# The last feed-forward by Strassen's 2x2 block product, with the closing norm on turned token tiles

## The chip, the cores and the metric

The kernel runs on one core of one Trainium2 chip. The metric is the device time of one execution in microseconds. Engines are TensorE (PE, with its weight loads as PEld), VectorE (DVE), ScalarE (ACT), GpSimd (POOL) and SyncE (SP), whose queue issues most DMAs.

## The reference, cut to what matters

Two layers, 1024 tokens of width 1024, all in float32. Layer 0 has a short gated convolution, layer 1 an attention with forget gates; each layer ends with a gated feed-forward of hidden width 2816, and each sub-layer with a norm.

```python
D_MODEL, SEQ, D_FF = 1024, 1024, 2816

def swiglu(h, w_gate, w_up, w_down):
    return (jax.nn.silu(h @ w_gate) * (h @ w_up)) @ w_down

for l in range(2):
    sh1, sc1, g1, sh2, sc2, g2 = jnp.split(c_act @ w_ada[l] + b_ada[l], 6, axis=-1)
    h = x * (1 + sc1) + sh1
    y = short_conv_mixer(h, ...) if l == 0 else forgetting_attention(h, ...)
    x = layer_norm(ALPHA * x + g1 * y, ln1_g[l], ln1_b[l])
    h = x * (1 + sc2) + sh2
    y = swiglu(h, ffn_w_gate[l], ffn_w_up[l], ffn_w_down[l])
    x = layer_norm(ALPHA * x + g2 * y, ln2_g[l], ln2_b[l])
```

## The kernel before, in words

Activations lie features on partitions: `x[k, half]` is 128 features by 512 tokens. Every large product splits both operands into a rounded part and the rest and adds three products (`mm3`, L166; its matmuls are L169 to L171), each 128x128 weights by 128x512. SBUF is cut into 47 pages of 512 KB, lent between classes ("h", "w", "hid", "att", and "f" for the Strassen stages); PSUM has six banks for products and two small ones. What stands where on each engine's queue is set by a recording layer that orders the program's steps by priority and data; `weave` mixes two lists of steps.

The first feed-forward (`first_ffn`, `hidden`, `down`) uses a Strassen form with seven products M1 to M7 for two by two blocks. The hidden width is taken in 11 pairs of 128-feature blocks. In `hidden`, a slot is one product of one pair for gate (m = 0) and up (m = 1), 12 matmuls each. For the first six pairs (`NEARLY`) M1 and M2 run ahead, in 12 slots that are woven with the norm's second half; the other slots follow. Blocks of weights come through a list of loads (`lq`), are added on GpSimd (L918 to L923), split by `split_f` (L659 on ScalarE, L660 on VectorE), and the activation sums T are made once by `sums_tail` (L681 to L745). `out` adds what is needed to a bank, applies SiLU to the gate and multiplies it with up:

```python
                nc.vector.tensor_tensor(y, bank, other, op=ALU.add)     # L999
                gp.tensor_tensor(y, y, a, op=ALU.mult)                  # L1000
```

`derive` makes the differences of hidden blocks that the down product needs (GpSimd, L1008), and `store` (L868) writes them to DRAM from SyncE's queue. From slot 28 on, each slot also loads a page of modulation weights and multiplies it in on VectorE (`ada_slot`, L260 and L262). `down` reloads the hidden blocks in three chunks and adds each of seven products times four row blocks to x (L1321).

The last feed-forward (`last_ffn`) has the plain form. Gate and up are taken block by block (`expand`), `ffn_evac` multiplies (L391 to L393). After the first chunk, x is turned to tokens on partitions (`to_token_major`, 64 transposes, L1375), so that the down product (`token_item`, L1400) and the closing norm (`token_norm`) work on 128 tokens by 512 features: per token tile two squares with their sums on ScalarE (L1423), the power on GpSimd (L1427, L1428), scale and shift on VectorE (L1417, L1434), or for one half ScalarE (L1437) and GpSimd. Its weights go through `Weights` (L147 and L153). Between attention and this stage, `self.rest` holds the last items of attention's output product (L423) and the first half's norm; the second half's norm (`ln_steps(1, ltail)`) is woven into the first products.

## Time and profile before

| | us |
|---|---|
| median of 3 runs | 2519.61 (2512.10 to 2519.83) |
| the profiled execution | 2518.77 |
| its span, first to last instruction | 2517.0 |
| TensorE busy | 2400.4 (95%) |
| VectorE busy | 1497.8 (60%) |
| ScalarE, GpSimd busy | 827.3 (33%), 860.0 (34%) |
| mean granted clock of TensorE | 0.981 of full speed |

Busy times are of one profiled execution; the program's own time is its span and a little around it. Matmuls overlap, so the busy time of a group of matmuls is more than the time that they hold the engine.

### The profile page before, as it was taken

What the parts mean: (1) busy time and instruction counts of PE and PEld (TensorE: products, weight loads), DVE (VectorE), ACT (ScalarE), POOL (GpSimd) and SP (SyncE); (2) the same over time, 40 slices, a digit from 0 to 9 for tenths busy, and PEclk for the clock granted to TensorE, in tenths of its full rate; (3) what the DMA queues carried; (4) which work ended last, traced back from release to release, by engine and by line L of the source; (5) the groups of instructions that cost most, each with busy time, mean ns of one, the idle gap of its engine ahead of it and who ended that gap; (6) DMA issues with size and microseconds to landing.
All of it is one profiled execution on the core that took longest, in us unless ns stands there. A gap on an engine that the chain in (4) does not pass through costs nothing. (4 is left out here: it accounts for less than half of the span.)

```text
span 2517.0 us, 29595 instructions
## 1 busy us (share of the span) xinstructions
PE 2400.4 (95%) x10905; PEld 1948.8 (77%) x10905; DVE 1497.8 (60%) x2129; ACT 827.3 (33%) x1321; POOL 860.0 (34%) x686
## 2 busy tenths in 40 slices
PE   7899999898899999999999999999999999999997
PEld 5688887687778878777777777777788888888886
DVE  5654548856788878986464667897632223232326
ACT  3311105421232333434223666665521111212113
POOL 6300002675556452343000556557330202030304
PEclk9999999999999999999999999999999999999999
DMA  8333303655575774215557555652211111111101
GB/s 269 118 101 117 92 17 97 202 163 173 174 225 173 272 249 147 83 51 194 192 179 226 174 176 145 153 133 72 67 34 51 51 51 51 51 43 50 44 32 67
DMA packets 286645, 311.95 MB, mean 124 GB/s; under 512 B 16068, under 2 KB 198548, under 8 KB 286500
## 3 DMA queue, kind: packets, MB, share of 16 engines
q1 hardware_dynamic: 274884, 284.69, 37.1%
q10 hardware_dynamic: 11616, 25.37, 2.7%
q8 instruction: 86, 1.41, 0.2%
q14 instruction: 59, 0.48, 0.1%
HBM read 252.91 MB, written 57.08 MB: 123 GB/s over the span
## 5 line engine op out<-in xcount | busy, mean ns | idle before, releaser
L169 PE MATMUL mm<-pg,pg 128*128 128x512 f32 x3004 | 1188.8, 397 | 35.8 <-DVE tA L979 11.4
L170 PE MATMUL mm<-pg,pg 128*128 128x512 f32 x3004 | 1186.1, 395 | 14.5 <-DVE pg L370 7.2
L171 PE MATMUL mm<-pg,pg 128*128 128x512 f32 x3004 | 1183.8, 394 | 3.6 <-POOL pg L368 2.6
L169 PEld LDWEIGHTS mm<-pg,pg 128*128 128x128 f32 x3004 | 571.7, 190 | 161.7 <-issue 18.2
L170 PEld LDWEIGHTS mm<-pg,pg 128*128 128x128 f32 x3004 | 571.8, 190 | 136.2 <-DVE pg L370 10.0
L171 PEld LDWEIGHTS mm<-pg,pg 128*128 128x128 f32 x3004 | 571.3, 190 | 125.2 <-POOL pg L368 4.1
L159 ACT CAST pg<-pg 128x1024 fp32r<-128x1024 f32 x144 | 150.5, 1052 | 586.2 <-PE mm L170 301.1
L660 DVE TENSOR_TENSOR pg<-pg,pg 128x1024 fp32r<-128x1024 f32 (+1 forms) x161 | 245.5, 1535 | 59.0 <-ACT pg L659 34.3
L1402 POOL TENSOR_TENSOR pg<-pg,tB 128x512 f32<-128x512 f32 x80 | 107.6, 1346 | 463.0 <-DVE tB L1400 462.1
L659 ACT CAST pg<-pg 128x1024 fp32r<-128x1024 f32 (+1 forms) x161 | 159.7, 1013 | 285.6 <-DVE pg L660 81.6
L163 DVE TENSOR_TENSOR pg<-pg,pg 128x1024 fp32r<-128x1024 f32 x124 | 154.2, 1248 | 151.9 <-ACT pg L159 149.4
L393 DVE TENSOR_TENSOR tB<-mm,tA 128x512 f32<-128x512 f32 x44 | 30.4, 692 | 215.9 <-PE mm L171 215.7
L262 DVE SCALAR_TENSOR_TENSOR ga<-pg,cact,ga 128x512 f32<-128x512 f32 x119 | 115.0, 966 | 53.9 <-DMA pg<-in_w_ada_dram 40.3
L1400 DVE TENSOR_TENSOR tB<-mm,pg 128x512 f32<-128x512 f32 x96 | 66.2, 690 | 134.7 <-PE mm L171 134.6
L1788 POOL TENSOR_SCALAR pg<-pg,st 128x512 f32<-128x512 f32 (+7 forms) x128 | 97.9, 773 | 122.1 <-DVE st L1786 116.3
L1811 DVE TENSOR_TENSOR pg<-sm,pg 128x512 fp32r<-128x512 f32 x192 | 104.1, 551 | 26.6 <-ACT pg L1810 23.8
L1810 ACT CAST pg<-sm 128x512 fp32r<-128x512 f32 x192 | 89.0, 480 | 50.8 <-PE sm L1807 48.7
L1785 ACT ACTIVATE pg<-s,st 128x512 f32<-128x512 f32 (+7 forms) x128 | 94.5, 744 | 28.3 <-DVE st L1782 19.1
L1779 DVE TENSOR_REDUCE st<-s 128x1 f32<-128x1024 f32 (+3 forms) x96 | 91.2, 951 | 15.1 <-PE s L1773 14.5
L1807 PE MATMUL sm<-ident,pg 128*128 128x128 f32 x576 | 98.6, 276 | 1.6 <-POOL pg L1788 1.3
L1190 POOL TENSOR_TENSOR pg<-pg,pg 128x1024 f32<-128x1024 f32 (+1 forms) x24 | 61.6, 2574 | 100.5 <-DVE pg L660 38.9
L1819 PE MATMUL mm<-pg,pg 128*128 128x512 f32 x192 | 80.3, 418 | 5.9 <-ACT pg L1810 4.7
(217 smaller groups left out, 2376.5 us busy)
## 6 DMA issues: line engine op xcount, KB each, us to landing
pg<-in_w_ada_dram SPq DMA_DIRECT2D x68, 512.0 KB
scr_hid<-pg SPq DMA_DIRECT2D x77, 256.0 KB
pg<-scr_hid SPq DMA_DIRECT2D x35, 512.0 KB
g<-in_w_ada_dram SPq DMA_DIRECT2D x56, 256.0 KB
pg<-in_ffn_w_gate_dram SPq DMA_DIRECT2D x56, 256.0 KB
pg<-in_ffn_w_up_dram SPq DMA_DIRECT2D x56, 256.0 KB
pg<-in_conv_w_in_dram SPq DMA_DIRECT2D x24, 512.0 KB
pg<-in_ffn_w_down_dram SPq DMA_DIRECT2D x44, 256.0 KB
```

What stands on the lines that cost most here:

```text
L159: nc.scalar.copy(hi, raw)
L163: nc.vector.tensor_tensor(lo, raw, hi, op=ALU.subtract)
L169: mm(out, lhsT=whi, rhs=xhi, start=first, stop=False, skip_group_check=skip)
L170: mm(out, lhsT=whi, rhs=xlo, start=False, stop=False, skip_group_check=skip)
L171: mm(out, lhsT=wlo, rhs=xhi, start=False, stop=last, skip_group_check=skip)
L262: eng.scalar_tensor_tensor(acc, w, s, acc, op0=ALU.mult, op1=ALU.add)
L659: nc.scalar.copy(hi[:, 0:n], flat[:, 0:n])
L660: nc.vector.tensor_tensor(lo[:, 0:n], flat[:, 0:n], hi[:, 0:n], op=ALU.subtract)
L1402: nc.gpsimd.tensor_tensor(z, z, m, op=ALU.add)
L1788: nc.gpsimd.tensor_scalar(lg[:, i], lg[:, i], s[:, i:i + 1], 1.0, op0=ALU.mult, op1=ALU.mult)
L1807: nc.tensor.transpose(p[:, j * P:(j + 1) * P], lg[j][:, kt * P:(kt + 1) * P], self.c["ident"])
L1811: nc.vector.tensor_tensor(pt[:, 1, a:], p[:, a:], pt[:, 0, a:], op=ALU.subtract)
```

## The change

The last feed-forward uses the same Strassen code as the first: `ffn_ahead` and `ffn_run` are the former `first_ffn_ahead` and the first part of `first_ffn`, now for layer l. x stays features on partitions to the end; `token_steps` turns each token tile after its last update, gets the mean by a product with a column of 1/1024 and norms the tile out of PSUM. The first token half's norm is woven with the last eight products, the second half's follows the last product. In `out` and `derive`, which both feed-forwards use, GpSimd's multiplications and differences go to VectorE. Layer 1 has no modulation slots.

```diff
@@ out, derive (in hidden, both layers)
-                gp.tensor_tensor(y, y, a, op=ALU.mult)
+                nc.vector.tensor_tensor(y, y, a, op=ALU.mult)
...
             def tt(n, o, a, b, op=ALU.subtract):
-                gp.tensor_tensor(o, a, b, op=op)
-                if n:
-                    store(n, j, o)
+                nc.vector.tensor_tensor(o, a, b, op=op)
+                store(n, j, o)
@@ run (in hidden)
-            queue(2, len(slots), self.adaq_lq((len(slots) - nada) // 4))
+            queue(2, len(slots), self.adaq_lq((len(slots) - nada) // 4) if l == 0 else [])
...
-                if i >= nada:
+                if i >= nada and l == 0:
                     self.ada_slot()
@@
-    def first_ffn_ahead(self):
+    def ffn_ahead(self, l):
         for k in range(KD):
-            self.drop("h", self.h.pop((k, 1)))
-        self.gather("h", "w", "raw")
+            if (k, 1) in self.h:
+                self.drop("h", self.h.pop((k, 1)))
+        self.gather("h", "w", "raw") if l == 0 else self.gather("h")
...
-        self.hidden_begin, self.hidden_run = self.hidden(0, NEARLY, False)
+        self.hidden_begin, self.hidden_run = self.hidden(l, NEARLY, False)
         self.hidden_begin()
@@
-    def to_token_major(self, half):
...
-    def token_item(self, half, t, c, ck, fs, gate, last):
...
-    def token_norm(self, half, t, sums, G, B, end):
...
+    def token_steps(self, half, t, G, B, mean, bank, end):
...
+        def turn():
+            box["p"] = [bank(), bank()]
+            for k in range(KD):
+                x = self.x[k, half][:, tok]
+                nc.tensor.transpose(box["p"][k // 4][:, k % 4 * P:(k % 4 + 1) * P], x, self.c["ident"])
+            for k in range(KD):
+                nc.tensor.matmul(mean[:, t:t + 1], lhsT=self.x[k, half][:, tok], rhs=self.c["ones"][:, 0:1],
+                                 start=k == 0, stop=k == KD - 1)
         def stats():
...
+            nc.vector.tensor_scalar(nm, mean[:, t:t + 1], -1.0, None, op0=ALU.mult)
             for c in range(2):
                 m = self.t("tmp", [P, HALF], tag="tA", bufs=3)
-                nc.scalar.activation(m, zs[c], AF.Square, bias=nm, accum_out=q[:, c:c + 1])
+                nc.scalar.activation(m, box["p"][c], AF.Square, bias=nm, accum_out=q[:, c:c + 1])
...
     def last_ffn(self, pre):
...
+        gen, nlast, _ = self.ffn_run(1, self.mod(1, 5), pre)
+        for ci, n, o in gen:
+            if (ci, n, o) == (nlast, "M6", 3):
+                G, B = self.fpage((P, 1024)), self.fpage((P, 1024))
                 self.spread_row(G, self.c["g"][2, 1], math.sqrt(D))
                 self.spread_row(B, self.c["b"][2, 1])
...
+            if (ci, n, o) == (nlast, "M4", 3):
+                break
+        one = lambda: next(gen)
+        mean = self.bank()
+        norm = [self.token_steps(0, t, G, B, mean, lambda: self.ps("sm"), False) for t in range(4)]
+        self.weave(([one] * 8, 0.0, 1.0), ([f for n in norm for f in n], 0.05, 1.0))
...
+        norm = [self.token_steps(1, t, G, B, mean, self.bank if t < 2 else lambda: self.ps("sm"), t > 1)
+                for t in range(4)]
+        for a, i in ((0, 0), (1, 0), (0, 1), (2, 0), (1, 1), (0, 2), (2, 1), (3, 0), (1, 2), (2, 2), (3, 1), (3, 2)):
+            norm[a][i]()
@@ build
-        vecs = self.ln_vectors(1, 1, m(1, 4), m(1, 3))
+        vecs = self.sums_vectors(1, 1, m(1, 4), m(1, 3))
...
-        self.lend("att", "w", 4)
-        self.queue_ffn(1, LAST_CHUNKS)
...
-        ltail = self.ln_tail(vecs)
+        ltail = self.sums_tail(vecs)
         for k in range(KD):
             ltail(k, 0)
+        self.ffn_ahead(1)
         for f in self.rest:
             f()
-        self.W.pump()
+        assert not self.W.queue
         pre = self.ln_steps(1, ltail)
         self.last_ffn(pre)
```

Three places show how the instructions move. The first is one pair in the first feed-forward's hidden stage. GpSimd before: L918 to L923 are weight sums, L1000 multiplications by the gate, L1008 differences.

```order
L921 TENSOR_TENSOR pg_4086<-pg_4086,pg_3972 128x1024
L918 TENSOR_TENSOR pg_4126<-pg_4126,pg_4129 128x1024
L1000 TENSOR_TENSOR tB_4122<-tB_4122,tA_4107 128x512
L1008 TENSOR_TENSOR pg_4047<-tB_4122,pg_4047 128x512
L923 TENSOR_TENSOR pg_3972<-pg_3932,pg_3972 128x1024
L919 TENSOR_TENSOR pg_4169<-pg_4126,pg_4169 128x1024
L1000 TENSOR_TENSOR pg_4163<-pg_4163,tA_4148 128x512
L1008 TENSOR_TENSOR pg_4163<-pg_4163,pg_4047 128x512
```

VectorE now, in the same pair (L958, L978 additions from a bank mm, L979 the multiplication, L987 the differences, L941 an addition that keeps a bank's sum, L639 a split):

```order
L958 TENSOR_TENSOR tA_4148<-mm_688_4055,pg_3993 128x512
L978 TENSOR_TENSOR pg_4163<-mm_690_4070,pg_3993 128x512
L979 TENSOR_TENSOR pg_4163<-pg_4163,tA_4148 128x512
L639 TENSOR_TENSOR pg_4210<-pg_4086,pg_4209 128x1024
L987 TENSOR_TENSOR pg_4163<-pg_4163,pg_4047 128x512
L941 TENSOR_TENSOR pg_4190<-mm_706_4177,pg_4089 128x512
L987 TENSOR_TENSOR pg_4047<-pg_4163,pg_4047 128x512
L941 TENSOR_TENSOR pg_4190<-mm_708_4192,pg_4089 128x512
```

On GpSimd a weight sum stood behind the gating of the product before; on VectorE the gating and the differences now stand between additions that free a bank and splits.

The second place is SyncE's queue where attention ends. Before, attention's last two output weights stand ahead of the feed-forward's weights:

```order
L1736 DMA pg_13846<-scr_f 3x1024
L1737 DMA pg_13847<-scr_v 128x8x128
L153 DMA pg_14226<-in_attn_w_o_dram 128x1024
L153 DMA pg_14232<-in_attn_w_o_dram 128x1024
L147 DMA pg_14447<-in_ffn_w_gate_dram 128x8x128
L147 DMA pg_14453<-in_ffn_w_up_dram 128x8x128
```

Now:

```order
L1664 DMA pg_13848<-scr_f 3x1024
L1665 DMA pg_13849<-scr_v 128x8x128
L660 DMA pg_14465<-in_ffn_w_gate_dram 128x4x128
L660 DMA pg_14465<-in_ffn_w_up_dram 128x4x128
L153 DMA pg_14228<-in_attn_w_o_dram 128x1024
L153 DMA pg_14234<-in_attn_w_o_dram 128x1024
L660 DMA pg_14320<-in_ffn_w_gate_dram 128x4x128
L660 DMA pg_14320<-in_ffn_w_up_dram 128x4x128
```

One pair of feed-forward blocks moved ahead of attention's last two weights.

The third place is the end of ScalarE's queue, the closing norm (L1423, now L1385, squares with their sum; L1437, now L1397, the scaling). Before, for the last two token tiles:

```order
L1423 ACTIVATE tA_19101,st_19099<-pg_6176,st_19099 128x512
L1423 ACTIVATE tA_19103,st_19099<-pg_6325,st_19099 128x512
L1437 ACTIVATE pg_6325<-pg_6325,st_19099 128x512
L1423 ACTIVATE tA_19143,st_19141<-pg_6178,st_19141 128x512
L1423 ACTIVATE tA_19145,st_19141<-pg_6327,st_19141 128x512
```

Now, for the last four, all behind the last product:

```order
L1385 ACTIVATE tA_19317,st_19314<-mm_3348_19278,st_19314 128x512
L1385 ACTIVATE tA_19319,st_19314<-mm_3349_19279,st_19314 128x512
L1385 ACTIVATE tA_19345,st_19342<-mm_3350_19296,st_19342 128x512
L1385 ACTIVATE tA_19347,st_19342<-mm_3351_19297,st_19342 128x512
L1397 ACTIVATE pg_19315<-mm_3349_19279,st_19314 128x512
L1385 ACTIVATE tA_19362,st_19359<-sm_19324,st_19359 128x512
L1385 ACTIVATE tA_19364,st_19359<-sm_19325,st_19359 128x512
L1397 ACTIVATE pg_19343<-mm_3351_19297,st_19342 128x512
L1385 ACTIVATE tA_19402,st_19399<-sm_19370,st_19399 128x512
L1385 ACTIVATE tA_19404,st_19399<-sm_19371,st_19399 128x512
```

The squares read PSUM banks (mm, sm) in place of pages, and eight of them follow the last product where two did.

## Rows read from the trace of the kernel before

**Rows 1.** The page: its span, and TensorE's busy time.
```profile
span 2517.0 us, 29595 instructions
PE 2400.4 (95%) x10905; PEld 1948.8 (77%) x10905; DVE 1497.8 (60%) x2129; ACT 827.3 (33%) x1321; POOL 860.0 (34%) x686
```
**Rows 2.** Timeline of TensorE, 431 to 434: start, us, engine, line, operation.
```profile
431.05 0.39 PE L169 MATMUL mm<-pg,pg 128*128 128x512 f32 x1
...
434.00 0.39 PE L170 MATMUL mm<-pg,pg 128*128 128x512 f32 x1
```
**Rows 3.** Timeline of VectorE: attention's last output update.
```profile
1768.09 0.75 DVE L423 SCALAR_TENSOR_TENSOR pg<-mm,mods,pg 128x512 f32<-128x512 f32 x1
```
**Rows 4.** Windows: us, PE, PEld, DVE, ACT, POOL busy (x), clock, DMA, GB/s.
```profile
414.00:891.00 477.00, 444.86 (x1905) 361.72 (x1904) 365.84 (x378) 150.95 (x200) 280.98 (x143) 0.96 0.59 195
891.00:1121.00 230.00, 219.87 (x950) 178.19 (x949) 193.80 (x207) 88.47 (x101) 84.06 (x40) 0.99 0.36 123
1768.00:2503.40 735.40, 731.13 (x3266) 604.13 (x3264) 243.03 (x325) 154.81 (x224) 149.39 (x125) 1.00 0.16 49
2503.40:2517.00 13.60, 0.00 (x0) 0.00 (x0) 7.46 (x13) 3.41 (x9) 5.82 (x8) 0.67 0.25 97
```
**Rows 5.** Windows within the first feed-forward's hidden stage.
```profile
440.00:520.00 80.00, 70.58 (x299) 56.58 (x298) 65.60 (x69) 33.34 (x48) 52.74 (x26) 0.96 0.62 199
520.00:560.00 40.00, 40.00 (x178) 33.11 (x177) 21.41 (x22) 9.65 (x11) 30.46 (x17) 1.00 0.40 130
560.00:720.00 160.00, 141.65 (x583) 114.92 (x582) 111.23 (x113) 36.21 (x44) 92.43 (x47) 0.93 0.60 194
720.00:760.00 40.00, 40.00 (x181) 33.10 (x181) 32.56 (x33) 12.16 (x17) 23.41 (x12) 1.00 0.56 179
```
**Rows 6.** Waits, 640 to 705, on SyncE and VectorE: us in total, times, longest.
```profile
SPq L868 <- POOL pg L1008: 21.5, 7, 11.9
...
DVE ga L262 <- DMA pg<-in_w_ada_kv_dram: 11.8, 2, 7.8
```
**Rows 7.** Windows of single lines: L1000, L1008, L262, L660, in this order.
```profile
414.00:921.00 507.00, 61.33 (x33) 0.96 0.59 197
414.00:921.00 507.00, 69.93 (x44) 0.96 0.59 197
414.00:891.00 477.00, 88.00 (x84) 0.96 0.59 195
414.00:891.00 477.00, 132.87 (x81) 0.96 0.59 195
```
**Rows 8.** Single lines: duration ns min/median/max, first and last start.
```profile
L443 DVE TENSOR_TENSOR tB<-pg,pg x4: 692/1518/1755, 373.9 to 1762.4; 128x512 f32<-128x512 f32 x4
L660 DVE TENSOR_TENSOR pg<-pg,pg x161: 675/1225/3422, 399.0 to 1094.1; 128x1024 fp32r<-128x1024 f32 x147, 128x512 fp32r<-128x512 f32 x14
L918 POOL TENSOR_TENSOR pg<-pg,pg x11: 2393/2713/3117, 466.2 to 833.2; 128x1024 f32<-128x1024 f32 x11
```
**Rows 9.** Timeline of TensorE: the last matmul.
```profile
2502.97 0.39 PE L171 MATMUL mm<-pg,pg 128*128 128x512 f32 x1
```
**Rows 10.** The chain that ended last: start us, us, what.
```profile
1784.17 1.07 PE sm L483 x8
...
1819.48 7.16 PE mm L1375 x64
...
2496.99 1.53 ACT tA L1423 x4
...
2509.72 0.71 ACT tA L1423 x2
...
2512.05 0.75 DVE pg L1434
```
**Rows 11.** Timeline of SyncE's queue where attention ends.
```profile
1729.81 2.71 SPq L153 DMA_DIRECT2D pg<-in_attn_w_o_dram  x2
...
1745.32 0.37 SPq L147 DMA_DIRECT2D pg<-in_ffn_w_gate_dram  x1
```

More of the change, by code (lines that the diff above doesn't have):

```diff
@@ L1430, in finish @@
         def finish():
+            st, z = box["st"], box["z"]
+            nm, rs = st[:, 0:1], st[:, 4:5]
             t0 = half * HALF + t * P
+            if not end:
+                nc.gpsimd.tensor_tensor(st[:, 1:2], nm, rs, op=ALU.mult)
+                nc.scalar.activation(z[:, 1], box["p"][1], AF.Identity, scale=rs, bias=st[:, 1:2])
+                nc.gpsimd.tensor_tensor(z[:, 1], z[:, 1], G[:, cs[1]], op=ALU.mult)
+                nc.gpsimd.tensor_tensor(z[:, 1], z[:, 1], B[:, cs[1]], op=ALU.add)
@@ L1440, in finish @@
[L1440 to L1465 removed]
+                    nc.vector.scalar_tensor_tensor(z[:, c], z[:, c], rs, B[:, cs[c]], op0=ALU.mult, op1=ALU.add)
@@ L1469, in last_ffn @@
-            for half in range(2):
-                W.pump()
-                for t in range(4):
-                    sums = self.t("small", [P, 2], tag="sums", bufs=2) if last else None
-                    self.token_item(half, t, 0, ck, fs, gate, sums)
-                    if finish:
-                        center()
-                    self.token_item(half, t, 1, ck, fs, gate, sums)
-                    end, before = half == 1 and t == 3, finish
-                    if finish and not end:
-                        finish()
-                    if last:
-                        stats, center, finish = self.token_norm(half, t, sums, G, B, end)
-                        stats()
-                    if before and end:
-                        before()
@@ L1491, in queue_block @@
+        assert next(gen, None) is None and not self.lq
+        self.unbank(mean)
+        mean = self.bank()
+        norm = [self.token_steps(1, t, G, B, mean, self.bank if t < 2 else lambda: self.ps("sm"), t > 1)
+                for t in range(4)]
+        for a, i in ((0, 0), (1, 0), (0, 1), (2, 0), (1, 1), (0, 2), (2, 1), (3, 0), (1, 2), (2, 2), (3, 1), (3, 2)):
+            norm[a][i]()
     def queue_block(self, chunks, srcs, csrc):
```

118 lines of the change are left out of this document (18 added, 100 removed).

## The prediction

> **What bounds the kernel now.** I read the page first, then busy time by stage, then waits, then single groups and stretches in order of time. TensorE is busy 95% of a span of 2517.0 us [rows 1]; the profiled execution took 2518.77 us, so 1.8 us lie outside the span, and that time is 0.8 us under the median of the runs, 2519.61. Busy time alone says little, because neighbouring matmuls overlap: one lasts 0.39 us, but from 431.05 to 434.00 thirteen starts pass in 2.95 us [rows 2]. So a 128x512 matmul costs 0.227 us when nothing is in its way.
>
> The last feed-forward begins when attention's last update is issued, at 1768.1 [rows 3], and its last matmul starts at 2502.97 [rows 9]. In this stage the reader sees TensorE busy 731 of 735 us at full clock, VectorE 243, GpSimd 149, DMA at 16% [rows 4]. The plain form has 22 blocks x 2 halves x 2 weights x 24 = 2112 matmuls up and 8 x 2 x 22 x 3 = 1056 down: 3168 x 0.227 = 719 us. With 64 transposes (7.2 us [rows 10]), spread rows and a norm's small matmuls, nearly all of the 735 is TensorE's own work. Fewer matmuls are the only thing that can shorten it.
>
> The same kernel has the Strassen form already, in the first feed-forward: hidden products from 414 to 891 and down products from 891 to 1121 [rows 4]. That is the template. It has 77 x 24 = 1848 and 7 x 4 x 11 x 3 = 924 matmuls, at 0.227 us 419.5 and 209.7 us; it took 477 and 230. So Strassen's form loses some 57 and 20 us there. The granted clock is 0.96 of full speed in the first part and 0.99 in the second: a stall costs twice, since a share of the time around it runs at 1.2 instead of 2.4 GHz.
>
> Where? A saturated stretch holds 181 matmul records in 40 us, 4.52 per us [rows 5]. From 440 to 520, where the norm's second half and the seven activation sums are made, 299 records are worth 66 us of 80: 14 lost. From 520 to 560 nothing is lost, with GpSimd at 30 of 40 us. From 560 to 720, where the modulation vectors' weights are loaded and multiplied in, 583 records are worth 129 of 160: 31 lost. About 7 more are scattered, and the modulation's transposes take 48 x 0.11 = 5. In the bad stretch VectorE waits 11.8 us for modulation weights, while the DMA queue of SyncE stands 21.5 us behind stores that wait for GpSimd's differences [rows 6].
>
> **The change, part by part.**
>
> *Fewer matmuls.* 3168 become 2772: 396 x 0.227 = 90 us off the path, if the new stage were as saturated as the old.
>
> *Hidden stage.* 419.5 us, plus 3 for the norm's small matmuls, plus stalls. The 14 us of the norm phase come again, since the same sums are built by the same code; I take all of it. The 31 us belong to a stretch with modulation work, and the last feed-forward has none: VectorE is spared 88 us of multiply-adds [rows 7], DMA the loads for them. I bound them by 0 (the clean stretch at 520) and 31 (all repeated), and take 3, near the clean stretch, which has the same early pairs and no modulation loads. Of the 7 scattered I take 6. Together 446 us. VectorE there: the first one's 366 us [rows 4] less 88 plus the moved work (below, 53) is 331 of 446, so it is not the bound.
>
> *Down stage.* 230 us as in the first one, less some 3 for its norm's small matmuls, plus the first token half's norm, which is woven into the last eight products: 32 transposes at 0.11 and 32 one-column products at 0.134 (eight take 1.07 us [rows 10]), 8 us. Together 235.
>
> *Closing norm.* Before, the span ends 13.6 us after the last matmul [rows 4]; only one token tile is left by then. Now four are. After the last product: the update 0.75 [rows 3] and its hand-over, 0.95; the transposes still open and eight one-column products 1.5; the negated mean and its hand-over 0.5, a guess; on ScalarE four tiles' squares with their read-outs, 1.53 a tile, and two scalings, taken as long as a square, 7.6 in a row; from the last square's end (2509.72 + 0.71) to the finishing pass at 2512.05, GpSimd's power, 1.6; two finishing passes 1.4; from their end to the span's end 3.5 [rows 10]. Sum 17.1, so 3.5 more. The bounds are 13.6 (only the last tile shows, as before) and 23 (four times 1.53 again, if each tile's squares also wait out the tile before).
>
> *The start.* Before, the first four block products covered only part of the norm of the second half. Now twelve products, 288 x 0.227 = 65 us, stand beside it. This is inside the 14 us above. The first weight pair now stands in SyncE's queue ahead of attention's last two output weights, which were issued at 1729.81 [rows 11]; if its page comes free late, the output projection slips. I cost it at nothing, because TensorE still has attention's last values in hand then; with that cover gone it is up to 15 us, the gap from 1729.8 to the third feed-forward weight load at 1745.3 [rows 11].
>
> *Gating and differences moved to VectorE*, in both feed-forwards. In the first, 33 multiplications (61.3 us) and 44 differences (69.9 us) leave GpSimd [rows 7]: 131 of its 281 us. On VectorE such an operation takes 0.69 us alone, the shortest of L443 [rows 8], 77 x 0.69 = 53 us; if each met GpSimd it would take up to 1.76, its longest, 135 us. I take 53, as GpSimd keeps only 150 of 477 us. In the first feed-forward VectorE goes from 366 to 419 of 477. Less collision with GpSimd gives some back: the splits there average 132.87 / 81 = 1.64 us [rows 7] against a median of 1.23 over the kernel [rows 8], 34 us in excess, of which about half goes. What stands behind the moved operations on VectorE are the operations that empty TensorE's banks, later by up to 1.4 us each time; what comes earlier are the stores, so SyncE's 21.5 us of standing shrink. I take -3 us for the first feed-forward, between -12 and +15.
>
> The Trainium skill (SBUF — State Buffer, section "Who interferes with whom") speaks against this step: a VectorE instruction with two SBUF inputs and a GpSimd instruction that reads SBUF cannot run together, and the second waits for the whole of the first. By that rule, with GpSimd busy 31% of the stage and half an operation of 2.7 us to wait out, each moved operation would cost some 0.4 us more, an estimate of 32 us for VectorE, which would stand at 451 of 477 us: the first feed-forward would then go to its upper bound, +15, and the sum to 2483. The trace agrees that collisions cost (0.69 us at best, 1.52 in the median, for L443 [rows 8]), but its clean stretch had GpSimd at 30 of 40 us, so the sum stays with the rows.
>
> *The sum*, against the profiled execution: 735.4 becomes 446 + 235 = 681, -54.4; the closing +3.5; the first feed-forward -3. 2518.8 - 53.9 = **2465 us**.
>
> **The rivals.**
>
> *Nearly no stalls.* GpSimd's relief removes most of the scattered stalls and a part of the first feed-forward's 31 us: -12 in the hidden stage, -9 more in the first one, 2444 us. For it: the clean stretch at 520. Against: 14 us arise before the first gating.
>
> *The first one's stalls come back.* The 31 us are not the modulation's but those of page reuse and block loads; +28, and VectorE crowds the first one for +15 rather than -3, +18: 2511, and 2483 or 2493 with one of the two. For it: VectorE at 88% there. Against: 40 us at full rate without modulation.
>
> *The gain doesn't come.* The stalls come back (+28), attention's output weights are late (+15) and the first feed-forward loses 8 rather than winning 3 (+11): 2519. Fewer matmuls, no shorter time. Against: the saturated rows, 4.52 records per us in Strassen's form [rows 5] and 4.44 in the plain one (3266 in 735.4 [rows 4]).
>
> *Slower: VectorE becomes the bound.* The place is the moved work in both hidden stages. Free time on VectorE is 477 - 366 = 111 us in the first and 446 - 278 = 168 in the last. With c us for each of 77 operations the excess is 77c - 111 and 77c - 168; together they eat 54 us from c = 2.15 us. At 2.7 + 0.69 = 3.4, every operation waiting out a whole weight sum of GpSimd (median 2.71 [rows 8]), the excess is 151 + 94 and the time 2710. Against it: the longest such operation here took 1.76, which gives 24.5 and nothing, 2490. The rule of the Trainium skill's page SBUF — State Buffer, section "Who interferes with whom", is the mechanism at its worst; no run here shows it for every operation.
>
> **How the numbers follow.** About 0.3%, 7.6 us, is what a measurement of this kernel can tell from no change. The forecast has 0.62 (2449 to 2483), nearly no stalls 0.13 (2437 to 2449), returning stalls 0.13 (2483 to 2511), the gain that doesn't come 0.06, VectorE as the bound 0.06. Faster by over 0.3% takes in the first three, less a hundredth for the top of the third: 0.87. No change 0.06, slower 0.07. The range takes the first two whole and the lower part of the third: 2437 to 2500.
>
> **What would show it.** Right: the last feed-forward's hidden part about 446 us, with its losses in the first 100 us and the clock near 0.98; VectorE about 330 us there; down about 235; a closing of 17 to 18 us led by ScalarE's squares; GpSimd's first hidden stage near 150 us and the first feed-forward's length within a dozen us. Wrong: a clean hidden part under 435, waits of TensorE for VectorE's bank-emptying operations through all pairs, splits longer than 1.64 us, or a gap before attention's output projection.

## The result, and the profile after

| | time, us (median, range) | ratio to before [95% interval] | span of the profiled execution |
|---|---|---|---|
| before | 2519.22 (4 runs) | | 2517.0 |
| after | 2444.62 (2441.51 to 2448.01, 4 runs) | 0.971 [0.9689, 0.9732] | 2442.3 |

The change wins 75 us where 54 were forecast; 2444.6 lies in the range, and on the rival *nearly no stalls* rather than on 2465. The page of the changed kernel begins (compare [rows 1]):

```profile
span 2442.3 us, 29959 instructions
...
PE 2325.3 (95%) x10629; PEld 1886.7 (77%) x10629; DVE 1773.7 (73%) x2382; ACT 912.9 (37%) x1407; POOL 791.7 (32%) x590
```

TensorE is still busy 95%, VectorE rose from 1498 to 1774 us, GpSimd fell from 860 to 792. Where the 75 us came from is read off five marks on VectorE and TensorE: the first update of each down stage, the last of the first feed-forward, attention's last, and the last 128x512 matmul. In the timeline of the changed kernel (start, us, engine, line, operation):

```profile
870.36 2.06 DVE L1300 SCALAR_TENSOR_TENSOR pg<-mm,mods,pg 128x512 f32<-128x512 f32 x3
...
1091.95 0.74 DVE L1300 SCALAR_TENSOR_TENSOR pg<-mm,mods,pg 128x512 f32<-128x512 f32 x1
...
1738.80 0.74 DVE L415 SCALAR_TENSOR_TENSOR pg<-mm,mods,pg 128x512 f32<-128x512 f32 x1
...
2187.57 1.39 DVE L1300 SCALAR_TENSOR_TENSOR pg<-mm,mods,pg 128x512 f32<-128x512 f32 x2
...
2418.13 0.39 PE L171 MATMUL mm<-pg,pg 128*128 128x512 f32 x1
```

Before, the first three stood at 893.9, 1120.8 and 1768.1 [rows 3]; the last feed-forward had no such down stage, and the last matmul stood at 2502.97 [rows 9]. The updates of the first down stage in the kernel before (duration ns min/median/max, first and last start):

```profile
L1321 DVE SCALAR_TENSOR_TENSOR pg<-mm,mods,pg x92: 735/745/751, 893.9 to 1120.8; 128x512 f32<-128x512 f32 x92
```

So attention ends 29.3 us earlier, of which 23.5 are won by 870.4, in the first feed-forward's hidden stage, 5.3 in its down stage and nothing behind it. From attention's last update to the end it takes 703.5 us instead of 748.9, 45.4 less. **In these two executions the last feed-forward, which the change is named for, gave 45 us; the first one, which it only touches, gave 29.** In the runs below with the same code up to there (e7, e8, e11) 22.5 to 23.2 of the 23.5 us come again, but only 0.7 to 3.3 of the 5.3.

The windows that answer to [rows 4] (us, then busy time and count of PE, PEld, DVE, ACT, POOL, the granted clock, DMA share, GB/s):

```profile
414.00:870.00 456.00, 439.87 (x1928) 358.19 (x1929) 404.65 (x454) 151.62 (x200) 164.01 (x71) 0.99 0.64 210
867.00:1092.00 225.00, 215.99 (x936) 175.61 (x935) 194.95 (x209) 86.84 (x98) 70.75 (x35) 0.98 0.35 115
1738.00:2190.00 452.00, 437.19 (x1900) 358.34 (x1899) 306.86 (x317) 154.47 (x200) 153.84 (x68) 0.98 0.49 163
2190.00:2420.00 230.00, 221.17 (x1016) 182.65 (x1015) 170.94 (x179) 81.27 (x99) 58.79 (x38) 0.98 0.30 102
```

The first hidden stage holds GpSimd for 164 us instead of 281 and VectorE for 405 instead of 366. The last hidden stage has VectorE at 307 us. The gain of the first one sits in one stretch, as the windows that answer to [rows 5] show:

```profile
440.00:520.00 80.00, 71.06 (x301) 56.32 (x300) 67.97 (x70) 32.86 (x47) 52.26 (x25) 0.96 0.63 201
520.00:560.00 40.00, 40.00 (x178) 33.14 (x177) 33.71 (x34) 10.64 (x12) 13.78 (x6) 1.00 0.55 176
560.00:720.00 160.00, 155.81 (x691) 127.21 (x691) 149.69 (x169) 42.43 (x52) 43.87 (x18) 1.00 0.65 208
```

The norm's stretch, 440 to 520, kept its loss (301 records, 299 before). The modulation's stretch, 560 to 720, holds 691 matmul records where it held 583: at 4.52 per us, 7 us lost instead of 31. VectorE is busy there 149.7 of 160 us (111.2 before) and waits almost nowhere. Its waits for the modulation's loads were 26 us in the same stretch before, the 11.8 of [rows 6] and (waits of VectorE: us in total, times, longest)

```profile
DVE ga L260 <- DMA pg<-in_w_ada_dram: 8.0, 1, 8.0
DVE ga L262 <- DMA pg<-in_w_ada_dram: 6.1, 1, 6.1
```

and are now

```profile
DVE ga L262 <- DMA pg<-in_w_ada_dram: 2.9, 1, 2.9
DVE ga L260 <- DMA pg<-in_w_ada_dram: 2.8, 1, 2.8
...
DVE ga L262 <- DMA pg<-in_w_ada_kv_dram: 1.0, 1, 1.0
```

### The profile page after: what moved, and what is told of

The parts are those of the page before. It is cut to its first block, busy times and chain, and to the rows that moved or that the text cites. A ratio compares the mean times of both kernels' runs of the same rounds, so it can differ in the third digit from the quotient of the medians.

```text
span 2442.3 us, 29959 instructions
## 1 busy us (share of the span) xinstructions
PE 2325.3 (95%) x10629; PEld 1886.7 (77%) x10629; DVE 1773.7 (73%) x2382; ACT 912.9 (37%) x1407; POOL 791.7 (32%) x590
## 5 line engine op out<-in xcount | busy, mean ns | idle before, releaser
L169 PE MATMUL mm<-pg,pg 128*128 128x512 f32 x2872 | 1139.2, 398 | 45.2 <-ACT pg L936 13.5
L170 PE MATMUL mm<-pg,pg 128*128 128x512 f32 x2872 | 1133.0, 395 | 10.5 <-DVE pg L370 6.7
L171 PE MATMUL mm<-pg,pg 128*128 128x512 f32 x2872 | 1133.1, 395 | 4.8 <-POOL pg L368 2.5
L169 PEld LDWEIGHTS mm<-pg,pg 128*128 128x128 f32 x2872 | 547.1, 191 | 171.6 <-ACT pg L936 18.3
L170 PEld LDWEIGHTS mm<-pg,pg 128*128 128x128 f32 x2872 | 547.0, 190 | 124.2 <-DVE pg L370 9.0
L171 PEld LDWEIGHTS mm<-pg,pg 128*128 128x128 f32 x2872 | 546.1, 190 | 122.4 <-POOL pg L368 4.1
L639 DVE TENSOR_TENSOR pg<-pg,pg 128x1024 fp32r<-128x1024 f32 (+1 forms) x322 | 462.6, 1446 | 97.9 <-ACT pg L638 55.6
L638 ACT CAST pg<-pg 128x1024 fp32r<-128x1024 f32 (+1 forms) x322 | 319.6, 1013 | 527.8 <-PE mm L171 150.9
L1168 POOL TENSOR_TENSOR pg<-pg,pg 128x1024 f32<-128x1024 f32 (+1 forms) x48 | 122.2, 2551 | 273.6 <-DMA pg<-in_ffn_w_down_dram 107.1
L1300 DVE SCALAR_TENSOR_TENSOR pg<-mm,mods,pg 128x512 f32<-128x512 f32 x184 | 134.7, 745 | 57.1 <-PE mm L171 56.9
L159 ACT CAST pg<-pg 128x1024 fp32r<-128x1024 f32 x78 | 81.5, 1051 | 208.8 <-PE mm L170 149.0
L262 DVE SCALAR_TENSOR_TENSOR ga<-pg,cact,ga 128x512 f32<-128x512 f32 x119 | 103.0, 866 | 38.6 <-DMA pg<-in_w_ada_dram 36.1
L1739 DVE TENSOR_TENSOR pg<-sm,pg 128x512 fp32r<-128x512 f32 x192 | 104.1, 551 | 26.4 <-ACT pg L1738 23.8
L959 ACT ACTIVATE tA<-tA 128x512 f32<-128x512 f32 x66 | 41.7, 632 | 188.9 <-DVE tA L958 188.8
L900 POOL TENSOR_TENSOR pg<-pg,pg 128x1024 f32<-128x1024 f32 x22 | 55.8, 2538 | 171.7 <-DMA pg<-in_ffn_w_up_dram 95.3
L1738 ACT CAST pg<-sm 128x512 fp32r<-128x512 f32 x192 | 89.0, 479 | 50.9 <-PE sm L1735 49.0
L163 DVE TENSOR_TENSOR pg<-pg,pg 128x1024 fp32r<-128x1024 f32 x58 | 70.8, 1226 | 41.6 <-ACT pg L159 41.2
L897 POOL TENSOR_TENSOR pg<-pg,pg 128x1024 f32<-128x1024 f32 x22 | 54.1, 2459 | 131.1 <-DMA pg<-in_ffn_w_up_dram 97.3
```

Source lines behind the costliest of these rows:

```text
L169: mm(out, lhsT=whi, rhs=xhi, start=first, stop=False, skip_group_check=skip)
L170: mm(out, lhsT=whi, rhs=xlo, start=False, stop=False, skip_group_check=skip)
L171: mm(out, lhsT=wlo, rhs=xhi, start=False, stop=last, skip_group_check=skip)
L262: eng.scalar_tensor_tensor(acc, w, s, acc, op0=ALU.mult, op1=ALU.add)
L638: nc.scalar.copy(hi[:, 0:n], flat[:, 0:n])
L639: nc.vector.tensor_tensor(lo[:, 0:n], flat[:, 0:n], hi[:, 0:n], op=ALU.subtract)
```

## The experiments

Ratios are to the kernel before on the same chip; marks are read from the one profiled execution of each run. One thing limits all of them: between programs that are identical up to attention's last update (after, e7, e8, e11), that mark stood at 1738.8, 1746.6, 1743.8 and 1747.5 us. Differences under some 10 us of the whole are therefore not put down to an edit, and stages are compared by their marks. Down's first update spreads less: 870.4, 870.7, 871.2 and 871.4 in the same four; 893.7 and 898.7 in e1 and e9, whose code is nearly the same.

### e1 to e4: what the moved gating is worth

In what follows, "the gating" is short for both kinds of moved operations, the multiplications and the differences. e1 puts them back on GpSimd in the changed kernel; e2 puts both on VectorE in the kernel before; e3 puts back the differences alone, e4 the multiplications alone.

```diff
# e1: both; e4: the first; e3: the second
-                nc.vector.tensor_tensor(y, y, a, op=ALU.mult)
+                gp.tensor_tensor(y, y, a, op=ALU.mult)
...
-                nc.vector.tensor_tensor(o, a, b, op=op)
+                gp.tensor_tensor(o, a, b, op=op)
```

> The changed kernel with the gating multiplications and the differences back on GpSimd, in both feed-forwards. Theory: the 29 us that the first feed-forward won come from these 77 operations per feed-forward, so attention's last update moves back from 1739 to about 1768 us, the last feed-forward loses a few us at most because it has no modulation work, and the time is 2474 to 2482 us. Rival: the first feed-forward won because the recording layer happened to order it otherwise, and the moved work is worth nothing: 2440 to 2450 us.

> The kernel before with the gating multiplications and the differences on VectorE, nothing else: the plain last feed-forward stays. Theory: the first feed-forward's hidden part shortens by some 23 us and its down part by some 5, as in the changed kernel, and the time is about 2490 us. Rival (moved work worth nothing by itself): 2515 to 2523 us.

> The changed kernel with only the differences back on GpSimd; the multiplications stay on VectorE. Theory: what hurts on GpSimd is its queue as a whole, where weight sums and stores stand behind 131 us of extra work, so giving back 70 of the 131 us gives back about half: 2455 to 2465 us. Rival: only the multiplication counts, since it stands first in the chain from the bank to the store: 2443 to 2449 us.

> The changed kernel with only the multiplications back on GpSimd; the differences stay on VectorE, behind them. Theory (GpSimd's queue as a whole): about half of the 29 us come back, 2455 to 2465 us. Rival (only the multiplication counts): nearly all come back, and VectorE waits for GpSimd besides: 2470 to 2485 us.

| | time, us | ratio to before [interval] | down's first update | attention's last | from there to the end |
|---|---|---|---|---|---|
| before | 2519.4 | | 893.9 | 1768.1 | 748.9 |
| e2: before, gating on VectorE | 2492.7 | 0.9891 [0.9874, 0.9907] | 870.2 | 1746.0 | 749.3 |
| e1: after, gating on GpSimd | 2478.1 | 0.9838 [0.9823, 0.9853] | 893.7 | 1766.5 | 708.1 |
| e4: multiplications on GpSimd | 2465.1 | 0.9779 [0.9765, 0.9794] | 892.3 | 1762.5 | 701.2 |
| e3: differences on GpSimd | 2452.7 | 0.9733 [0.9718, 0.9747] | 878.5 | 1748.8 | 702.9 |
| after | 2444.6 | 0.971 [0.9689, 0.9732] | 870.4 | 1738.8 | 703.5 |

The two parts of the change separate, as far as the spread lets one see. Strassen's form in the last feed-forward is worth 41 us (e1), the gating on VectorE 27 in the kernel before (e2) and 33 behind Strassen's form. The marks say where: **the part of the gating's gain that repeats, some 23 us, lies in the first feed-forward's hidden stage** (893.7 against 870.4, and 893.9 against 870.2 in e2); the last part takes 701 to 708 us with the gating on either engine. The 5 us that e2 was expected to win in the first down stage did not come (226.8 us, 226.9 before). Of the two kinds the multiplications matter most: by the total, e4 ends at the upper edge of its theory and e3 between its two ranges, but at down's first update e4 gives back 21.9 of e1's 23.3 us and e3 8.1, more than that mark spreads. Together that is more than 23.3, so the two shares do not simply add.

### How GpSimd's gating held up TensorE

The stretch 560 to 720 of e1 loses as much as that of the kernel before (584 records; e9, with the same order of GpSimd's operations there, has 553, so some 30 records are spread; with the gating on VectorE there are 691 to 694 in all five programs):

```profile
560.00:720.00 160.00, 141.14 (x584) 114.53 (x584) 113.49 (x113) 35.67 (x43) 93.34 (x47) 0.93 0.61 194
```

One stall of it, on the timeline of e1; the last bracket of a row is the idle time before it and what ended it:

```profile
576.00 2.28 POOL L979 TENSOR_TENSOR tB<-tB,tA 128x512 f32<-128x512 f32 x1
...
578.36 1.29 POOL L987 TENSOR_TENSOR pg<-tB,pg 128x512 f32<-128x512 f32 x1
...
579.68 10.02 SPq L847 DMA_DIRECT2D scr_hid<-pg  x4
...
586.68 2.66 POOL L987 TENSOR_TENSOR pg<-pg,pg 128x512 f32<-128x512 f32 x2
...
589.80 5.94 SPq L762 DMA_DIRECT2D pg<-in_w_ada_dram  x3
...
594.07 0.49 DVE L260 TENSOR_SCALAR ga<-pg,cact 128x512 f32<-128x512 f32 x1 [8.03 <-DMA pg<-in_w_ada_dram]
...
595.86 1.28 DVE L941 TENSOR_TENSOR pg<-mm,pg 128x512 f32<-128x512 f32 x2
...
596.69 0.76 PE L169 MATMUL mm<-pg,pg 128*128 128x512 f32 x1 [3.16 <-DVE pg L941]
```

GpSimd's difference ends at 579.65, behind a multiplication that took 2.28 us. Two weight sums and another multiplication follow on GpSimd, and the next two differences end only at 589.34. The stores of these results stand in SyncE's queue, four in 10.0 us, the last issued at 589.37, and only then come the modulation's loads, at 589.80. VectorE's multiply-add waits 8.03 us for the first of them, the additions that empty banks (L941) stand behind it in VectorE's queue, and TensorE waits 3.16 us for those. That is one chain. A second price is in the same trace: VectorE's operations with two SBUF inputs are stretched while GpSimd works. The groups of lines in 560 to 720, of e1 and then of the changed kernel (count | busy us, mean ns of one | idle before):

```profile
L639 DVE TENSOR_TENSOR pg<-pg,pg 128x1024 fp32r<-128x1024 f32 x24 | 43.1, 1797 | 20.1 <-ACT pg L638 15.7 <-PE mm L170 1.9 <-DMA pg<-in_ffn_w_up_dram 1.9
L262 DVE SCALAR_TENSOR_TENSOR ga<-pg,cact,ga 128x512 f32<-128x512 f32 x35 | 39.9, 1140 | 17.4 <-DMA pg<-in_w_ada_kv_dram 11.0 <-DMA pg<-in_w_ada_dram 5.7
L958 DVE TENSOR_TENSOR tA<-mm,pg 128x512 f32<-128x512 f32 x14 | 9.5, 681 | 1.0 <-PE mm L171 1.0
```

```profile
L262 DVE SCALAR_TENSOR_TENSOR ga<-pg,cact,ga 128x512 f32<-128x512 f32 x42 | 39.1, 932 | 4.5 <-DMA pg<-in_w_ada_dram 2.9 <-DMA pg<-in_w_ada_kv_dram 1.0
L639 DVE TENSOR_TENSOR pg<-pg,pg 128x1024 fp32r<-128x1024 f32 x27 | 36.2, 1340 | 2.2 <-PE mm L170 1.8 <-ACT pg L638 0.3
...
L958 DVE TENSOR_TENSOR tA<-mm,pg 128x512 f32<-128x512 f32 x16 | 10.9, 683 | 0.0
```

A split (L639) takes 1797 ns against 1340 (1489 in e8, of the same code), a multiply-add (L262) 1140 against 932, while the addition that reads a bank (L958) takes 681 and 683. Sorted by the start and end times of the trace, the 61 splits of the changed kernel between 414 and 891 that overlapped no GpSimd operation took 1.21 to 1.23 us, the 26 that did 2.07 us on average and up to 3.42. The Trainium skill (SBUF — State Buffer, section "Who interferes with whom") says just that: two SBUF inputs collide with GpSimd's reads, one does not. And e4 shows a third price. There splits are stretched no more than in the changed kernel (1308 ns) and the loads are hardly late (8 us), yet 614 records are all the stretch holds, while the differences on VectorE wait in its queue for GpSimd's product (the stretch in e4, and waits of VectorE in it):

```profile
560.00:720.00 160.00, 144.68 (x614) 116.85 (x613) 103.61 (x132) 36.62 (x44) 59.85 (x31) 0.96 0.61 189
```

```profile
DVE pg L987 <- POOL pg L979: 25.0, 9, 6.1
DVE pg L987 <- POOL tB L979: 22.0, 5, 9.7
```

What TensorE itself waits for is mostly the same each way, VectorE's additions that empty its banks (L958, L941): 14.7 us in this stretch of e1, 13.0 in e4, 16.6 in e6, 4.0 in the changed kernel. Five more runs (e5, e6, e9, e10, e12) were to tell apart what makes VectorE late.

### e5, e10: as many operations on GpSimd, for nothing

```diff
+        def extra():
+            gp.tensor_tensor(d, d, d, op=ALU.mult)
...
                 nc.vector.tensor_tensor(y, y, a, op=ALU.mult)
+                extra()
...
                 nc.vector.tensor_tensor(o, a, b, op=op)
+                extra()
# e10: extra() does nothing in the first twelve steps (early products)
```

> The changed kernel, with one more GpSimd product of a 128x512 scratch tile with itself behind each of the 77 moved operations of a feed-forward: as many operations of the same size, on the engine they left, that wait for nothing and that nobody waits for. Theory (two queues in a ring: what cost the time when the gating stood on GpSimd was that it, and the stores behind it on SyncE's queue, waited behind weight sums that wait for loads): idle work lengthens nothing that is waited for, so 2445 to 2452 us, down's first update of the first feed-forward still at 870 to 876 us. Rival one (GpSimd's busy time itself, or the slower VectorE beside it, was the cost): as with the gating on GpSimd, 2468 to 2480 us, that update at 888 to 895 us.

> The idle GpSimd work again, one product of a 128x512 scratch tile with itself behind each moved operation, but only from the first step behind the early products on: before, the scratch tile took the norm's buffer, and the norm at the head of the feed-forward waited 46 us behind the idle work. Theory (what is waited for behind GpSimd's queue was the cost, not its busy time): 2443 to 2453 us, down's first update of the first feed-forward at 869 to 876 us. Rival (GpSimd's busy time, or the slower VectorE beside it): 2465 to 2480 us, that update at 886 to 895 us.

2588.9 us (ratio 1.0277 [1.026, 1.0295]) and 2564.7 (1.017 [1.0145, 1.0196]): far above every range that was expected, and no test of either side. Waiting for nothing, the idle work was ordered by the recording layer as early as its priority let it, in one heap at the head of the stage: e10's GpSimd runs eight scratch products in a row here, thirteen there, and is busy 19 of every 20 us from 460 to 580. What waited behind it were the activation sums that `sums_tail` makes at the head of the stage (waits of e10, 440 to 540: us in total, times, longest):

```profile
ACT pg L678 <- POOL pg L704: 34.8, 4, 11.0
```

What the two runs do show is GpSimd's queue as a cost of its own: work that nobody needs delays the operations queued behind it. Down's first update came at 949.0 and 932.5 us instead of 870.4.

### e6: the stores leave SyncE's queue

```diff
# on e1, in store()
-                nc.sync.dma_start(self.dr[n][j * P:(j + 1) * P], t)
+                gp.dma_start(self.dr[n][j * P:(j + 1) * P], t)
```

> The changed kernel with both kinds of moved operations back on GpSimd (2478 us), and their stores issued by GpSimd itself behind the operation, so that SyncE's queue, with the loads of weights and of the modulation behind the stores, no longer waits for GpSimd. Theory (the ring closes through SyncE's queue): most of the 33 us come back, 2447 to 2460 us, down's first update of the first feed-forward at 872 to 882 us, and the waits of the modulation's sums for their loads at most a third of those with the stores on SyncE. Rival one (VectorE slowed, or GpSimd too busy): 2472 to 2485 us, that update at 890 to 896 us. Rival two (issuing a store costs GpSimd more than the wait saved): above 2485 us.

2504.2 us (0.9934 [0.9912, 0.9956]), 26 us above e1. The waits for the modulation's loads in 560 to 720 fell to 4.9 us, as the theory wanted, and nothing came back: rival two in the total, with down's first update at 908.9 us. GpSimd issues 77 stores in the hidden stage in 44.0 us, and VectorE is stretched further (lines of e6, 560 to 720):

```profile
L639 DVE TENSOR_TENSOR pg<-pg,pg 128x1024 fp32r<-128x1024 f32 x25 | 47.1, 1885 | 23.7 <-ACT pg L638 21.1 <-PE mm L170 1.9 <-issue 0.6
L262 DVE SCALAR_TENSOR_TENSOR ga<-pg,cact,ga 128x512 f32<-128x512 f32 x35 | 46.1, 1316 | 5.6 <-DMA pg<-in_w_ada_dram 4.9
```

So the late loads are not what the 33 us hang on alone: without them, and with splits at 1885 ns, the stretch still holds only 604 records. The run changes two things at once, though: GpSimd, with the stores to issue, is busy 107.9 of the 160 us, where it was 93.3 in e1.

### e12: the modulation's loads ahead of the stores

```diff
# on e1
-                if i >= nada and ada:
+                if i >= nada - 3 and ada:
                     self.lq.append(ada.pop(0))
```

> The changed kernel with both kinds of moved operations back on GpSimd (2478 us), and the loads of the modulation in the first feed-forward queued three steps earlier, so that they stand ahead of the stores that wait for GpSimd. With the gating on GpSimd TensorE stalled between 560 and 720 us behind evacuations that stood behind a modulation's sum waiting for its load (3.2 and 4.2 us), and behind VectorE operations stretched while GpSimd worked (5.8 us). Theory (the late modulation loads are the greater part): 2448 to 2462 us, the sums' waits for those loads between 560 and 720 us below 8 us instead of 25, down's first update of the first feed-forward at 871 to 880 us instead of 893.7. Rival (VectorE stretched by GpSimd, and the gating's own lateness, are the greater part): 2470 to 2482 us with those waits gone all the same. Between 2462 and 2470 us: both, in about equal parts.

2491.8 us (0.9879 [0.9861, 0.9897]), 14 above e1 (905.1 at down's first update), which neither side foresaw. The waits for the modulation's loads fell from 25 to 16 us, and the weights of the products, pushed back in the same queue, came late instead (waits in 560 to 720):

```profile
ACT pg L638 <- DMA pg<-in_ffn_w_up_dram: 24.7, 3, 13.9
...
ACT pg L638 <- DMA pg<-in_ffn_w_gate_dram: 11.7, 1, 11.7
DVE ga L262 <- DMA pg<-in_w_ada_dram: 10.9, 2, 7.5
...
DVE ga L260 <- DMA pg<-in_w_ada_dram: 4.7, 1, 4.7
```

By these waits SyncE's queue is late as a whole when stores in it wait for GpSimd; the edit chose other loads to stand behind them.

### e9: weight sums behind the gating

```diff
# on e1: sums() leaves ahead(i) for the end of the step
-            return out + [lambda: self.flush(i)]
+            return out + [lambda: ahead_sums(i), lambda: self.flush(i)]
```

> The changed kernel with both kinds of moved operations back on GpSimd (2478 us), and the weight sums of a step issued behind the step's gating on GpSimd instead of ahead of it, so that the gating no longer stands behind sums that wait for their loads. Theory (GpSimd's queue: gating waits behind sums that wait for loads, and the stores and loads wait for the gating): a good part of the 33 us comes back, 2448 to 2464 us, down's first update of the first feed-forward at 872 to 884 us instead of 893.7. Rival one (GpSimd's busy time or the slower VectorE is the cost): 2472 to 2482 us, that update at 889 to 896 us. Rival two (the sums, now later, are what the splits wait for): 2485 us or more.

2486.1 us (0.9856 [0.9832, 0.9881]). This run tells nothing of its theory: the recording layer put GpSimd's operations in the stretch in the same order as in e1, with the sums where they were, so the kernel is e1 but for a few places in the stretch of the norm and the activation sums.

### e7: gating on GpSimd in the last feed-forward alone

```diff
-                nc.vector.tensor_tensor(y, y, a, op=ALU.mult)
+                (gp if l else nc.vector).tensor_tensor(y, y, a, op=ALU.mult)
# and the differences likewise
```

> The changed kernel, with the moved operations back on GpSimd in the last feed-forward alone; the first keeps them on VectorE. Theory (the move pays only where the modulation's loads and sums run beside the feed-forward; the last part was as long with either, 703.5 and 708.1 us): 2441 to 2450 us, attention's last update at 1738 to 1740 us. Rival (each feed-forward has its half of the 33 us): 2457 to 2465 us, and a last part 12 us or more longer than 703.5 us.

2457.0 us (0.9751 [0.9728, 0.9774]): by the total, at the lower edge of the rival's range. The marks decide. The last part took 703.8 us, as with the gating on VectorE (703.5); what its profiled execution is longer by, 8 us, is there at attention's last update already, up to which this program equals the changed kernel. It is the spread named above, and it also took the mark out of the theory's 1738 to 1740. From attention's last update to the last down stage's first it takes 447.5 us in e7 and 445.4 in e1, with the gating on GpSimd, and 446.9 to 448.8 in after, e8 and e11, with it on VectorE. In the last hidden stage, which has no modulation work, the move brings nothing.

### e8, e11: the closing norm

```diff
# e8
-        mean = self.bank()
-        norm = [self.token_steps(1, t, G, B, mean, ...
+        means = [self.bank(), self.bank()]
+        norm = [self.token_steps(1, t, G, B, means[t % 2], ...
# e11: also tile 3 into tile 0's banks, and all tiles but 0 scaled and shifted on VectorE
```

> The changed kernel, with the means of the second half's four tiles in two banks, in turn, instead of one. Theory (the first negated mean waited for the second tile's products because they write the same bank): the first negated mean is done within 0.6 us of its tile's last product instead of 2.4 us, and from the start of the last 128x512 product to the end it takes 21 to 23 us instead of 24.2. Rival (the wait is the order of the instructions on the engines, or the last tile's bank and GpSimd's queue hide it): 24 to 24.5 us. The whole run moves by less than one look can tell.

> The changed kernel with the means of the second half in two banks, in turn, the last tile turned into the first one's banks instead of the third's, and the second tile's closing gating on VectorE instead of ScalarE and GpSimd. Theory (the closing is long because the last tile waits for the third's banks, and its variance stands behind the second tile's gating on GpSimd): from the start of the last 128x512 product to the end 19 to 22 us instead of 24.2, 2440 to 2443 us. Rival (TensorE, in order and at a lower granted clock in the closing, sets its pace with the one-column products, as with two banks alone): 23.5 to 25 us, 2443 to 2448 us.

In the changed kernel, behind the last matmul (timeline; x is the number of records, two for each one-column product):

```profile
2421.80 1.84 PE L1375 MATMUL mm<-ones,pg 128*128 128x1 f32 x16
...
2423.68 0.16 DVE L1382 TENSOR_SCALAR st<-mm 128x1 f32<-128x1 f32 x1 [4.37 <-PE mm L1375]
...
2430.72 1.94 PE L1373 MATMUL sm<-ident,pg 128*128 128x128 f32 x8 [1.89 <-DVE pg L1387]
...
2436.11 0.73 POOL L1388 TENSOR_SCALAR st<-st 128x1 f32<-128x1 f32 x1
```

The first tile's negated mean (L1382) waited until 2423.68, for the second tile's products in the same bank; the last tile's turning (2430.72) 1.89 us for a bank; its variance (L1388) until 2436.11 on GpSimd. With two banks (e8, a single run: 2445.5 us) the first negated mean came 2.5 us earlier, counted from the last matmul; with all three edits (e11: 2449.7, 0.9713 [0.9692, 0.9734]) all these waits are gone. Yet from the start of the last matmul to the end it took 24.2 us in after, 24.2 in e8 and 24.0 in e11: in both runs the rival held. In e11 TensorE itself is what the others wait for. Its timeline, then its windows, then those of the changed kernel (the clock is the third number from the right):

```profile
2432.77 3.41 PE L1375 MATMUL mm<-ones,pg 128*128 128x1 f32 x16
```
```profile
2424.00:2428.00 4.00, 4.00 (x34) 3.75 (x33) 0.90 (x2) 0.00 (x0) 2.11 (x2) 1.00 0.33 131
2430.00:2440.00 10.00, 10.00 (x50) 10.00 (x51) 4.61 (x9) 3.56 (x9) 4.96 (x8) 0.50 0.15 57
```
```profile
2418.00:2428.00 10.00, 9.69 (x88) 9.47 (x86) 3.23 (x7) 2.90 (x9) 1.19 (x4) 1.00 0.08 29
2428.00:2442.00 14.00, 2.77 (x13) 2.31 (x12) 8.32 (x11) 4.23 (x10) 8.91 (x11) 0.50 0.39 150
```

One tile's eight one-column products take 3.41 us instead of 1.84, because the granted clock stood at 0.50 of full speed (1.2 GHz) by 2430, at most five us after the last large matmul (2424.80); in the changed kernel it held 1.00 until 2428, when all but the last tile's turning was done. A shorter wait earlier was paid back by products at half speed.

No version beat the changed kernel: e8 and e11 stand nearest, within the spread.

## Why the prediction was right, and where it was not

**Fewer matmuls, hidden and down stage: right.** With the mark that [rows 4] used, 2.9 us ahead of down's first update, the last hidden stage took 2184.7 - 1738.8 = 445.9 us for 446, and down 233.8 to the end of the last matmul for 235. VectorE stood at 307 us there for 331. The moved operations took 74.9 us of that for the 53 taken, so what else VectorE does there was put too high by 46. Most of the losses lie where they were put: 16 us in the first 102, where TensorE waits for the sums and the norm, none from 1840 to 2160; the last 30 us lose 8 more. e1, with the gating on GpSimd in both stages, gives 41 us for the forecast's 50.9; 7 of what is missing are the closing, below.

**The first feed-forward, -3 between -12 and +15: this step failed.** It won 29 us in the profiled execution, 23.5 of them in the hidden stage, where they come again in other runs of the same code. The failing piece is where the 31 us of the modulation's stretch were given to "the modulation work", as something that stays where the modulation is. 24 of them were the gating on GpSimd in company with that work: with the gating on VectorE and every load and multiply-add still there, 7 remain. That it takes the two together is concluded from the last hidden stage, where GpSimd's gating costs nothing (e1, e7); no run leaves the modulation out of the first. The prediction had read a row that pointed there, the 21.5 us in which SyncE's queue stood behind GpSimd's differences [rows 6], and wrote that it would shrink, but gave it no price. It had also read only 65 us of the stretch: over all 160 the queue stood 81 us behind GpSimd's gating (44.5 for differences, 36.7 for multiplications), and now stands 58 behind VectorE's (32.1 and 25.9), the longest time 5.0 us instead of 11.9. The chain from it to TensorE (stores, loads, multiply-add, bank-emptying addition) was not followed. Only the rival *nearly no stalls* held part of it, at -9; its -12 in the last hidden stage did not come, so it met the time by other terms than its own, which is luck. The stated range holds the measured time only because it reaches down over that rival.

**The price of the moved operations: mis-sized, and of no account.** In 414 to 891 of the changed kernel, the multiplications and the differences (windows of L979 and of L987):

```profile
414.00:891.00 477.00, 43.97 (x33) 0.99 0.64 210
...
414.00:891.00 477.00, 41.17 (x44) 0.99 0.64 210
```

85 us for 77, 1.1 each, where 53 were taken; the 32 us more are what the sum estimated from the Trainium skill's rule (SBUF — State Buffer, section "Who interferes with whom"). The trace agrees on where they come from: the 54 of the 77 that overlapped no GpSimd operation took 0.68 to 0.70 us, the 23 that did 2.1 on average. But its conclusion, +15 for the stage and 2483 in all, did not follow: the stage was 23.5 us shorter. In that estimate the collision was counted only for what moves. GpSimd's shorter queue gave back on the splits (1.47 us each in that window, 1.64 before: 14 us for 81, where the forecast had taken half of 34) and on the multiply-adds (76 us, 88 before), which had no term, and the waits went. VectorE reached 405 us in the stage, not 451. *VectorE becomes the bound* needed 2.15 us an operation; the longest single one took 2.90, beyond the 1.76 that the prediction had from four operations, but the mean was 1.1.

**The closing, 17.1: mis-sized by 6.7 us.** It took 23.8, just past the upper bound of 23. Two terms: the one-column products were priced at 0.134 each, from x8 records read as eight products, where two records make one; a tile's eight take 1.84, not 1.07, and four tiles' stand in a row on TensorE. And each tile's mean waited for the next tile's products and the last for banks, which the sum had put at a guessed 0.5. That ScalarE's squares lead was wrong: the last tile waited for a bank and for GpSimd's queue, and with those waits gone (e11) TensorE led, at half clock.

**The start, at nothing: right.** No gap opened before attention's output projection; from the first feed-forward's last update to attention's last it took 646.9 us, 647.3 before.

In the terms of the sum: -54.4 came as 445.9 + 233.8 - 735.3 = -55.6, +3.5 as 23.8 - 13.6 = +10.2, and -3 as -29.3. It was 21 us off, by a stage that the forecast had treated as nearly untouched.

**What stays open.** How the 24 us of the modulation's stretch divide among late loads, stretched VectorE operations and waits for GpSimd's products. They stand in for each other: e4 has the third almost without the other two and loses 17 of the 24, e6 has the second almost without the first, and a busier GpSimd, and loses 19 (614 and 604 records at 4.52 per us, against 691). No run took away just one, and 614, 604 and e1's 584 lie no further apart than e1 and e9. The first down stage's 5.3 us are not shown to belong to the gating either: e7, e8 and e11, with the same code there, took 226.2, 223.6 and 226.2 us and e2 226.8, the kernel before 226.9, and e4, with the multiplications on GpSimd, 221.5.

## What to carry to other kernels

When work leaves an in-order queue, price what stood behind it, link by link, up to the engine that sets the end; here operations on an engine busy 59% of a stage, which none of TensorE's waits in the stretch names (18.4 us, all behind VectorE), cost 24 us; the traces show stores in a DMA queue, loads behind them, collisions and waits for its results, not what each is worth. An engine's busy share does not say whether it can take more: VectorE went from 70% to 94% of the stretch and TensorE's stalls fell, as VectorE's waits went (those for late loads from 26 us to 7). Before an experiment that depends on an order, look at the order which the recording layer makes of it: three runs here (e5, e9, e10) did not test what they were written for.

## What the runs showed of the hardware

- VectorE operations with two SBUF inputs lengthen beside GpSimd, those with a bank as one input do not. Between 414 and 891 of the changed kernel, a moved operation took 0.68 to 0.70 us when no GpSimd operation overlapped it and up to 2.90 when one did, a split 1.21 to 1.23 and up to 3.42. In 560 to 720 a split took 1340 to 1489 ns on average (after, e8), 1600, 1797 and 1885 as more of the small work stood on GpSimd (e3, e1, e6; 1308 in e4, with the multiplications alone there), the bank-reading additions 678 to 684 throughout.
- A store issued by GpSimd cost that engine 0.57 us (44.0 us for 77 in e6).
- A one-column product makes two records of the profile and takes 0.23 us at full clock, as long as a 128x512 product of the large kind (0.227), and 0.43 at half.
- Behind the last large matmul the granted clock fell to 0.50 within five us in e8 and e11, though TensorE had no gap, with transposes and one-column products; in the changed kernel it fell at about 2428, ten us behind. There it had also stood at 0.50 from 2411 to 2414, behind another tile's transposes and one-column products, and was back at 1.00 from 2415 to 2418, behind large matmuls.
- In the last down stage a split beside one of GpSimd's weight sums, of 2.4 us each, took 3.04 us instead of 1.2, and TensorE stood 6.5 us until 2340.5 (timeline of the changed kernel); no run tried those sums elsewhere:

```profile
2329.53 2.40 POOL L1168 TENSOR_TENSOR pg<-pg,pg 128x1024 f32<-128x1024 f32 x1 [2.36 <-DVE pg L639]
...
2329.97 3.04 DVE L639 TENSOR_TENSOR pg<-pg,pg 128x1024 fp32r<-128x1024 f32 x1
...
2340.51 0.79 PE L169 MATMUL mm<-pg,pg 128*128 128x512 f32 x1 [6.50 <-DVE pg L1300]
```
